# A hybrid decoder layer on one core: x also loaded feature-major, the inverse norm spread by a transpose, projection weights laid out by block

## The chip, the cores and the metric

The kernel runs on one core of one Trainium2 chip. The core has five engines with a queue of instructions each: TensorE (PE, matmuls and transposes, writes to PSUM), VectorE (DVE), ScalarE (ACT), GpSimd (POOL), and SyncE (SP), which here issues the transfers. They wait for each other by semaphores. The metric is the device time of one execution in microseconds, median of several; lower is better.

## The reference

One layer with 1024 tokens and 16 learned meta tokens in front of them, model width 1024, float32. Only its beginning is touched:

```python
h = jnp.concatenate([meta, x], axis=1)
u = rmsnorm(h, attn_norm_w[l])          # x * rsqrt(mean(x*x) + eps) * w
proj = u @ w_in[l]
gq, gk, gv, gz, gb, ga, fq, fk, fv, ff = jnp.split(proj, IN_SPLITS, axis=-1)
...                                     # gated DeltaNet group, forgetting attention group
h = h + jnp.concatenate([o_gdn, o_fox], axis=-1) @ w_out[l]
h = h + swiglu(rmsnorm(h, ffn_norm_w[l]), w_gate[l], w_up[l], w_down[l])
```

## The kernel before

Each large product is made of three fast matmuls. A float32 operand is split into a high half (a cast by ACT, line 163) and a low half (the source minus the high half, a subtraction by DVE, line 164); `mm3` (lines 197 to 199) adds high x high, high x low and low x high for each of the eight 128-row blocks k of the contraction, so one output tile takes 24 matmuls.

The first stage makes the normed input u, feature-major and split (`uh`, `ul`: 128 partitions x 8 blocks x 1040 columns), and beside it one projection that needs tokens on the output's partitions: 256 columns of the z gate and 8 gate columns, `z1`. It goes over eight tiles of 128 tokens (t = 0 to 7), then the 16 meta tokens (t = -1). For each tile `load_norm` loads 128 rows of x, and `norm_to` works on them:

- ACT squares the rows and sums along them (line 251), DVE scales and adds eps (line 212, called the statistic here), POOL raises to the power -0.5 (line 213);
- DVE multiplies the rows by the inverse norm and the norm's weight, which lies broadcast over the partitions in `nwb` (line 254, `xn`);
- PE transposes `xn` in eight 128x128 pieces into two PSUM banks (line 261), and for each bank (half 0: k = 0 to 3, half 1: k = 4 to 7) ACT casts and DVE subtracts into `uh` and `ul`.

`proj_tm` then runs the 24 z matmuls of the tile. DVE copies the 8 gate columns (line 312), ACT applies Silu to the 256 z columns (line 301), POOL multiplies by a weight (line 302), SP stores the result. `zg` is the product for the meta tokens, 8 columns wide.

`win_block` loads 256 or 264 columns of the input projection's weights in two transfers of four blocks k each, rows of 1 KB, and splits each of the two (`whi`, `wlo`). After the first stage a loop over pairs of heads loads the gk, gq and gv blocks and runs `proj_fm`, 128 columns of weights stationary against 348 or 346 tokens (`pj_k` and so on); `xlds` (the x loads) and `casts` (the last cast and subtraction of each norm) order the gk weights behind the norm.

The program's text order is a priority: the framework places instructions in each engine's queue by it and by a model of their times, and each queue then runs in order. So matmuls of two tiles can stand interleaved in PE's queue. `tc.issue_after(ins)` puts an instruction behind `ins` in the queue of the engine that runs `ins`; it adds no semaphore. Twenty warm-up products of a matrix of ones (line 133, 40 matmul instructions) come first on PE.

## Time and profile before

| | us |
|---|---|
| median of three runs | 1322.56 |
| lowest and highest run | 1321.23, 1324.68 |
| profiled execution, first to last instruction | 1318.3 |
| what lies around that span, against the median | 4.3 |
| last meta product of the first stage on PE starts | 46.63 |
| first matmul of the unbroken run of the next projection starts | 46.90 |

The profiled execution is one run, seen from inside; its span has no time of its own beside it but the runs' median. In the rows of the profile a group's idle time stands behind a bar with what ended it; in the order of instructions each row has start, duration, engine, line, operation, output, inputs and shape. SPq is SP's queue of transfers; PEld the loading of stationary operands, beside the matmuls.

### The profile page before, as it was taken

How to read it: one execution, taken by the hardware profiler on the slowest of the kernel's cores; microseconds unless marked ns; L12 is line 12 of the kernel's file. 1: busy time of each engine (PE TensorE's matmuls, PEld its weight loads, DVE VectorE, ACT ScalarE, POOL GpSimd, SP SyncE). 2: the span in 40 equal slices, each digit the busy share in tenths (PEclk: the TensorE clock that was granted, in tenths of full speed). 3: DMA queues.
4: the chain of work that ended last, by engine and by line, in shares of the span. 5: the costliest groups of instructions: out<-in, count | busy, mean ns of one | idle time of the engine just before them, and what ended most of it. 6: DMA issues, size and time to landing. Idle time of an engine off the chain costs nothing.

```text
span 1318.3 us, 20034 instructions
## 1 busy us (share of the span) xinstructions
PE 1296.8 (98%) x7442; PEld 1132.9 (86%) x7442; DVE 856.0 (65%) x1525; ACT 546.2 (41%) x918; POOL 390.6 (30%) x348
## 2 busy tenths in 40 slices
PE   8999999999999999999999999999999999999997
PEld 8999999899999988887778888888888888888886
DVE  6665789676237578996897665566566665355644
ACT  5543434232223367885553332333323343333332
POOL 2211423601023321113432644554334453010301
PEclk9999999999999999999999999999999999999999
DMA  6331743774479597647444555534454557955513
GB/s 228 98 107 38 213 134 115 215 219 144 150 241 330 180 245 207 163 118 233 166 138 137 180 176 181 172 128 155 156 169 146 176 203 261 402 178 191 210 63 128
DMA packets 184777, 233.88 MB, mean 177 GB/s; under 512 B 19121, under 2 KB 136873, under 8 KB 181865
## 3 DMA queue, kind: packets, MB, share of 16 engines
q1 hardware_dynamic: 181704, 223.70, 52.7%
q0 software_dynamic: 2976, 8.92, 2.2%
q8 instruction: 58, 0.95, 0.3%
q14 instruction: 39, 0.31, 0.1%
HBM read 154.91 MB, written 77.67 MB: 176 GB/s over the span
## 4 chain that ended last, share of the span: by engine, by line
PE 82%; DVE 6%; DMA 5%; issue 3%; ACT 2%; POOL 1%; SPq 1%; POOLq 0%; DVEq 0%; ACTq 0%
PE xp L1545 9%; PE yp L1545 7%; PE gb L1379 5%; PE gd L1379 5%; PE ud L1379 5%; PE ub L1379 5%; PE ga L1379 4%; PE ua L1379 4%; PE pj_fk L207 4%; PE pj_fq L207 4%; PE pt L1012 2%; PE ge L1379 2%; PE ue L1379 2%; PE fv L207 2%; PE wog L207 2%
## 5 line engine op out<-in xcount | busy, mean ns | idle before, releaser
L164 DVE TENSOR_TENSOR al_p<-ra_p,ah_p 128x2048 fp32r<-128x2048 f32 (+1 forms) x21 | 46.6, 2221 | 94.0 <-ACT ah_p L163 94.0
L163 ACT CAST ah_p<-ra_p 128x2048 fp32r<-128x2048 f32 (+1 forms) x21 | 37.1, 1766 | 105.8 <-PE xp L1545 48.5
L1545 PE MATMUL xp<-wh_p,ah_p 128*128 128x512 f32 (+1 forms) x187 | 70.6, 377 | 0.7 <-DVE hs L1572 0.7
L1545 PE MATMUL xp<-wl_p,ah_p 128*128 128x512 f32 (+1 forms) x187 | 70.5, 377 | 0.0
L1545 PE MATMUL xp<-wh_p,al_p 128*128 128x512 f32 (+1 forms) x187 | 70.5, 377 | 0.0
L1432 POOL TENSOR_TENSOR gzw<-gzw,uzt 128x512 f32<-128x512 f32 x11 | 18.4, 1675 | 153.8 <-DVE uzt L1423 127.6
L1432 POOL TENSOR_TENSOR gxy<-gxy,uxy 128x512 f32<-128x512 f32 x22 | 39.0, 1772 | 67.2 <-DVE uxy L1423 48.2
L1379 PE MATMUL gb<-uh_p,w_g_p 128*128 128x512 f32 x176 | 57.8, 390 | 0.0
L1379 PE MATMUL gd<-uh_p,w_g_p 128*128 128x512 f32 x176 | 57.8, 389 | 0.0
L1379 PE MATMUL ub<-uh_p,w_u_p 128*128 128x512 f32 x176 | 57.8, 389 | 0.0
L1379 PE MATMUL ud<-uh_p,w_u_p 128*128 128x512 f32 x176 | 57.8, 389 | 0.0
L985 ACT ACTIVATE pr<-pr,sm 128x144 f32<-128x144 f32 (+3 forms) x64 | 50.6, 792 | 16.9 <-DVE sm L980 16.6
L164 DVE TENSOR_TENSOR w_u_p<-raw_u,w_u_p 128x512 fp32r<-128x512 f32 x42 | 42.8, 1018 | 21.6 <-ACT w_u_p L163 21.4
L164 DVE TENSOR_TENSOR pl<-pt,ph 128x512 fp32r<-128x512 f32 (+1 forms) x96 | 51.2, 553 | 2.2 <-ACT ph L163 1.6
L1379 PE MATMUL ga<-uh_p,w_g_p 128*128 128x512 f32 x160 | 52.5, 389 | 0.0
L1379 PE MATMUL ua<-uh_p,w_u_p 128*128 128x512 f32 x160 | 52.5, 389 | 0.0
L163 ACT CAST ph<-pt 128x512 fp32r<-128x512 f32 (+1 forms) x96 | 45.4, 474 | 14.7 <-PE pt L1012 13.9
L1545 PE MATMUL yp<-wl_p,ah_p 128*128 128x512 f32 x132 | 51.4, 390 | 0.0
L1545 PE MATMUL yp<-wh_p,ah_p 128*128 128x512 f32 x132 | 51.4, 389 | 0.0
L1545 PE MATMUL yp<-wh_p,al_p 128*128 128x512 f32 x132 | 51.4, 389 | 0.0
L164 DVE TENSOR_TENSOR wl_p<-rw_p,wh_p 128x2048 fp32r<-128x2048 f32 (+1 forms) x21 | 46.9, 2235 | 3.4 <-ACT wh_p L163 3.4
L1012 PE MATMUL pt<-ident,pr 128*128 128x128 f32 x288 | 48.1, 276 | 0.0
(638 smaller groups left out, 4272.3 us busy)
## 6 DMA issues: line engine op xcount, KB each, us to landing
ra_p<-ao_p SPq DMA_DIRECT2D x14, 1024.0 KB
raw_g<-in_w_gate_dram SPq DMA_DIRECT2D x22, 512.0 KB
raw_u<-in_w_up_dram SPq DMA_DIRECT2D x22, 512.0 KB
raw_d<-in_w_down_dram SPq DMA_DIRECT2D x22, 512.0 KB
wt_p<-raw_d SPq DMA_DIRECT2D x33, 256.0 KB
rw_p<-wt_p SPq DMA_DIRECT2D x8, 1024.0 KB
rw_p<-in_w_down_dram SPq DMA_DIRECT2D x6, 1024.0 KB
ao_p<-gzw SPq DMA_DIRECT2D x22, 256.0 KB
```

Of the source, the lines that this page charges most:

```text
L163: cast = nc.scalar.copy(dst_hi, src)
L164: tail[0] = (cast, nc.vector.tensor_sub(dst_lo, src, dst_hi.bitcast(F32)))
L207: nc.tensor.matmul(dst, a, b, start=first, stop=last)
L985: nc.scalar.activation(pr[:, :n], pr[:, :n], AF.Exp, bias=sm[:, np_ - 1:np_], scale=-1.0, accum_out=rsum[:, h, j:j + 1])
L1012: nc.tensor.transpose(pt[:rows_k, P * j:P * j + P], pts[j][0][:, c0:c0 + rows_k], ident)
L1379: nc.tensor.matmul(dst, a[:, c], b[:, k], start=(first and k == 0 and i == 0), stop=(k == 3 and i == 2), skip_group_check=not first)
L1432: last_mul[0] = G.tensor_tensor(gs[d], gs[d], us[d], op=ALU.mult)
L1545: nc.tensor.matmul(dst[:, n_], a[:, f, c], b[:, f, n_], start=(first and i == 0 and n == 0), stop=(i == NF - 1 and n == 2), skip_group_che ...
```

## The change

The host passes more and other layouts. x also comes as `x_t`, for each tile of 128 tokens feature-major (128 partitions x 8 blocks x 128 tokens), the meta tokens as `meta_t`, the norm's weight as eight columns, `attn_norm_w_t`. `w_in` comes as one flat array in the order in which blocks are used, so that a transfer of `win_block` reads one run of 4096 or 4224 bytes for each partition.

`norm_to` no longer makes `xn` nor transposes it. It still squares the token-major rows for the norm. PE transposes the column of inverse norms, broadcast over 128 columns, so that a PSUM tile `pr` holds the inverse norm of each token along the columns, the same in each partition. DVE then makes, for each k, feature-major x times the weight's column times `pr` (128x128 for a tile), and the halves are split from that. Tiles 4 and 5, and 6 and 7, are normed as pairs (128x256). The norm of the next tile or pair is called from inside the z matmuls (`mm3_behind`): after `cut` of them, its transpose is put behind the last one on PE, and the rest behind the transpose. Tile 0 takes its products with low weights last. Explicit orders put the square behind a cast of the tile ahead, the statistic behind a subtraction, the multiplies behind the tile ahead's last subtraction, and the second half of the z weights behind tile 0's.

```diff
@@ -28,6 +28,8 @@
 EPS = 1e-6
 WMAX = 1056
 GQ, GK, GV, GZ, FQ, FK, FV = 0, 512, 1024, 1536, 2056, 2568, 3080
+WIN = tuple((c, 256) for c in range(0, 1792, 256)) + ((1792, 264),) + tuple(
+    (c, 256) for c in range(2056, 3336, 256)) + ((3336, 264),)
 TCH = ((0, 348), (348, 346), (694, 346))
 GRP = 4
 LV0 = (76.0, 119.0)
@@ -95,12 +97,11 @@
 
 
 @with_exitstack
-def tile_hymba_layer(ctx, tc, x, meta, attn_norm_w, w_in, conv_w, a_log, dt_bias, gdn_norm_w,
+def tile_hymba_layer(ctx, tc, x, meta, x_t, meta_t, anw_t, attn_norm_w, w_in, conv_w, a_log, dt_bias, gdn_norm_w,
                      fgate_b, w_out, ffn_norm_w, w_gate, w_up, w_down, final_norm_w, out):
     nc = tc.nc
-    x, out, w_in, conv_w = x[0], out[0], w_in[0], conv_w[0]
+    x, out, conv_w = x[0], out[0], conv_w[0]
     w_out, w_gate, w_up, w_down = w_out[0], w_gate[0], w_up[0], w_down[0]
-    w_in_v = w_in.rearrange("(k p) n -> p k n", p=P)
 
     const = ctx.enter_context(tc.tile_pool(name="const", bufs=1))
     dram = ctx.enter_context(tc.tile_pool(name="dram", bufs=1, space=bass.MemoryType.DRAM))
@@ -182,11 +183,16 @@
 
     parts_n = [1]
 
-    def win_block(c0, n, name):
+    def win_block(c0, n, name, behind=None):
         ws = ([], [])
         for i in range(2):
-            k0 = KT // 2 * i
-            hl = load_w([(w_in_v[:, k0:k0 + KT // 2, c0:c0 + n], KT // 2 * n)], f"{name}_{i}")
+            k0, m = KT // 2 * i, KT // 2 * n
+            o = P * KT * c0 + P * m * i
+            src = w_in[o:o + P * m].rearrange("(p m) -> p m", m=m)
+            with ExitStack() as es:
+                for ins in behind if behind and i else ():
+                    es.enter_context(tc.issue_after(ins.ins))
+                hl = load_w([(src, m)], f"{name}_{i}")
             for o, t in zip(ws, hl):
                 o.extend(t[:, n * k:n * k + n] for k in range(KT // 2))
         return ws
@@ -197,6 +203,19 @@
             nc.tensor.matmul(dst, lh, rh, start=(first and i == 0), stop=False)
             nc.tensor.matmul(dst, lh, rl, start=False, stop=False)
             nc.tensor.matmul(dst, ll, rh, start=False, stop=(last and i == n - 1))
+
+    def mm3_behind(dst, pairs, cut, hook, lo_last):
+        ops = [[(lh, rh), (lh, rl), (ll, rh)] for lh, ll, rh, rl in pairs]
+        if lo_last:
+            h = len(ops) // 2
+            ops = ops[:h] + [[o[0] for o in ops[h:]], [o[2] for o in ops[h:]], [o[1] for o in ops[h:]]]
+        ops = [o for g in ops for o in g]
+        ins = None
+        for i, (a, b) in enumerate(ops):
+            if hook and i == cut:
+                ins = hook(mm)
+            with tc.issue_after(ins.ins) if ins else nullcontext():
+                mm = nc.tensor.matmul(dst, a, b, start=i == 0, stop=i == len(ops) - 1)
 
     od = PeOrder()
 
@@ -237,40 +256,70 @@
     pre = ExitStack()
     xp = pre.enter_context(tc.tile_pool(name="xp", bufs=3))
     xc = pre.enter_context(tc.tile_pool(name="xc", bufs=1))
-    nwb = xc.tile([P, D], F32, name="nwb")
-    x0 = xp.tile([P, D], F32, tag="xt", bufs=5, name="xt_0")
-    nc.sync.dma_start(x0, x[0:P])
-    nc.sync.dma_start(nwb, attn_norm_w[0].partition_broadcast(P))
-
     pows, xlds, casts = [], [], []
-
-    def norm_to(src, rows, wb, hi, lo, col, pool, nm):
-        junk = pool.tile([P, D], F32, tag="junk", name=f"jk_{nm}")
-        st = pool.tile([P, 4], F32, tag="st", name=f"st_{nm}")
-        with tc.issue_after(casts[-2][0].ins) if len(casts) > 2 else nullcontext():
-            nc.scalar.activation(junk[:rows], src[:rows], AF.Square, accum_out=st[:rows, 0:1])
-        pows.append(inv_rms(st[:rows, 2:3], st[:rows, 0:1], 1, 1.0 / D, st[:rows, 1:2]))
-        xn = pool.tile([P, D], F32, tag="xn", name=f"xn_{nm}")
-        nc.vector.scalar_tensor_tensor(xn[:rows], src[:rows], st[:rows, 2:3], wb[:rows],
-                                       op0=ALU.mult, op1=ALU.mult)
+    x_q, halves_ = {}, []
+
+    def load_x(t, n=1):
+        xg = xp.tile([P, n, KT, P], F32, tag=f"xg{n}", bufs=4 - n, name=f"xg_{t}")
+        if t < 0:
+            xg = xg.rearrange("p n k c -> p (n k c)")[:, :KT * NM].rearrange("p (n k c) -> p n k c", n=1, k=KT)
+        xts = [xp.tile([P, D], F32, tag="xt", bufs=6, name=f"xt_{t + i}") for i in range(n)]
+        lds = [(xts[0][:NM], meta), (xg[:, 0], meta_t)] if t < 0 else [
+            (xts[i], x[P * (t + i):P * (t + i) + P]) for i in range(n)] + [(xg[:, i], x_t[t + i]) for i in range(n)]
+        for d, src in lds:
+            with tc.issue_after(xlds[-1].ins) if xlds else nullcontext():
+                xlds.append(nc.sync.dma_start(d, src))
+        x_q[t] = xts, xg
+
+    load_x(0)
+    wct = xc.tile([P, KT], F32, name="wct")
+    nc.sync.dma_start(wct, anw_t)
+
+    def norm_to(t, behind=None):
+        col, rows = tok_cols(t)
+        xts, xg = x_q.pop(t)
+        n = len(xts)
+        pr = ps_t(f"pr_{t}")
+        un = xp.tile([P, KT, 2 * P], F32, tag="un", bufs=2, name=f"un_{t}")
+        if t < 2:
+            order = halves_[1:] if t < 0 else casts or [None]
+        else:
+            order = (casts[-2], halves_[0]) if t == 4 else tuple(halves_)
+        for i, xt in enumerate(xts):
+            st = xp.tile([P, 4], F32, tag="st", bufs=4, name=f"st_{t + i}")
+            if rows < P:
+                nc.gpsimd.memset(st, 1.0)
+            ahead = order[i]
+            with tc.issue_after(ahead[0].ins) if ahead else nullcontext():
+                nc.scalar.activation(un[:rows, 4 * i:4 * i + 4].rearrange("p k c -> p (k c)"), xt[:rows], AF.Square,
+                                     accum_out=st[:rows, 0:1])
+            with tc.issue_after(ahead[1].ins) if ahead else nullcontext():
+                pows.append(inv_rms(st[:rows, 2:3], st[:rows, 0:1], 1, 1.0 / D, st[:rows, 1:2]))
+            with tc.issue_after(behind.ins) if behind else nullcontext():
+                last_pr = nc.tensor.transpose(pr[:, P * i:P * i + P], st[:, 2:3].to_broadcast([P, P]), ident)
+        prv = pr[:, :rows * n].rearrange("p (n c) -> p n c", n=n)
+        un = un[:, :, :rows * n]
+        cols = slice(col, col + rows * n)
         for g in range(2):
-            pt = ps_t(f"pt_{nm}_{g}")
-            pv = pt.rearrange("p (a b) -> p a b", a=4)[:, :, :rows]
-            for i in range(4):
-                k = 4 * g + i
-                nc.tensor.transpose(pv[:, i, :], xn[:rows, P * k:P * k + P], ident[:rows, :rows])
-            split_dst = (hi[:, 4 * g:4 * g + 4, col:col + rows], lo[:, 4 * g:4 * g + 4, col:col + rows])
-            split(split_dst[0], split_dst[1], pv)
+            ks = slice(4 * g, 4 * g + 4)
+            for k in range(4 * g, 4 * g + 4):
+                with tc.issue_after(casts[-1][1].ins) if casts else nullcontext():
+                    nc.vector.scalar_tensor_tensor(un[:, k].rearrange("p (n c) -> p n c", n=n), xg[:, :, k],
+                                                   wct[:, k:k + 1], prv, op0=ALU.mult, op1=ALU.mult)
+            split(uh[:, ks, cols], ul[:, ks, cols], un[:, ks])
+            halves_[g:] = [tail[0]]
         casts.append(tail[0])
+        return last_pr
 
     def tok_cols(t):
         return (0, NM) if t < 0 else (NM + P * t, P)
 
-    def proj_tm(t, w, c0, n, name, tag=ps_mm):
+    def proj_tm(t, w, c0, n, name, cut=0, hook=None):
         col, rows = tok_cols(t)
-        acc = tag(name)
-        mm3(acc[:rows, :n], [(uh[:, k, col:col + rows], ul[:, k, col:col + rows],
-                              w[0][k][:, c0:c0 + n], w[1][k][:, c0:c0 + n]) for k in range(KT)])
+        acc = ps_mm(name)
+        mm3_behind(acc[:rows, :n], [(uh[:, k, col:col + rows], ul[:, k, col:col + rows],
+                                     w[0][k][:, c0:c0 + n], w[1][k][:, c0:c0 + n]) for k in range(KT)],
+                   cut, hook, t == 0)
         return acc
 
     def proj_fm(w, m0, c0, n, name):
@@ -284,14 +333,6 @@
     nc.gpsimd.memset(gt[:, NT], 0.0)
     nc.gpsimd.memset(fr[:, NT], 0.0)
     zp = pre.enter_context(tc.tile_pool(name="zp", bufs=2))
-    def load_norm(t):
-        rows = NM if t < 0 else P
-        if t:
-            xt = xp.tile([P, D], F32, tag="xt", bufs=5, name=f"xt_{t}")
-            xlds.append(nc.sync.dma_start(xt[:rows], meta if t < 0 else x[P * t:P * t + P]))
-        else:
-            xt = x0
-        norm_to(xt, rows, nwb, uh, ul, 0 if t < 0 else NM + P * t, xp, f"a{t}")
 
     gnw = gpool.tile([P, P], F32, name="gnw")
 
@@ -302,16 +343,21 @@
         nc.gpsimd.tensor_tensor(zt, zt, gnw[:, None, :].broadcast_to([P, 2, P]), op=ALU.mult)
         nc.sync.dma_start(rec_d[t, :, 7, h0:h0 + 2], zt)
 
-    w = None
+    norm_to(0)
+    w = win_block(GZ + 256, 264, "z1", casts[0])
+    casts[0] = tail[0]
+    for t in (1, 2, 3):
+        load_x(t)
+    nc.sync.dma_start(gnw, gdn_norm_w[0].partition_broadcast(P))
     for t in range(NT):
-        load_norm(t)
-        if w is None:
-            w = win_block(GZ + 256, 264, "z1")
-            nc.sync.dma_start(gnw, gdn_norm_w[0].partition_broadcast(P))
-        acc = proj_tm(t, w, 0, 264, f"z1_{t}")
+        if t in (0, 1):
+            load_x(2 * t + 4, 2)
+        elif t == 2:
+            load_x(-1)
+        nxt = {0: (1, 18), 1: (2, 18), 2: (3, 18), 3: (4, 18), 5: (6, 6), 6: (-1, 18)}.get(t)
+        acc = proj_tm(t, w, 0, 264, f"z1_{t}", *((nxt[1], lambda mm: norm_to(nxt[0], mm)) if nxt else ()))
         nc.vector.tensor_copy(gt[:, t], acc[:, 256:264])
         gate_out(t, acc, zp, "zt", 2)
-    load_norm(-1)
     acc = proj_tm(-1, w, 256, 8, "zg")
     nc.vector.tensor_copy(gt[:NM, NT], acc[:NM, :8])
     pre.close()
@@ -557,7 +603,7 @@
         kqs = [gp.tile([P, 2, T], F32, tag="kq", bufs=3, name=f"kq_{2 * hp + i}") for i in range(2)]
         vts = [gp.tile([P, T], F32, tag="vt", bufs=2, name=f"vt_{2 * hp + i}") for i in range(2)]
         with ExitStack() as es:
-            for ins in (xlds[-1], *casts[6]) if not hp else ():
+            for ins in (xlds[-1], *casts[5]) if not hp else ():
                 es.enter_context(tc.issue_after(ins.ins))
             w = win_block(GK + c, 256, f"gk{hp}")
         for i in range(2):
...
@@ -1646,8 +1692,14 @@
 
     nc = bacc.Bacc("TRN2", target_bir_lowering=False, num_devices=1, dynamic_dma_scratch_size=1024)
     arrays, args = {}, []
+    laid = dict(inputs)
+    laid["x_t"] = np.asarray(inputs["x"]).reshape(NT, P, KT, P).transpose(0, 3, 2, 1)
+    laid["meta_t"] = np.asarray(inputs["meta_tokens"]).reshape(NM, KT, P).transpose(2, 1, 0)
+    wi = np.asarray(inputs["w_in"])[0].reshape(2, KT // 2, P, -1)
+    laid["w_in"] = np.concatenate([wi[i, :, :, c:c + n].transpose(1, 0, 2).ravel() for c, n in WIN for i in range(2)])
+    laid["attn_norm_w_t"] = np.asarray(inputs["attn_norm_w"]).reshape(KT, P).T
     for name in _INS:
-        a = np.ascontiguousarray(inputs[name])
+        a = np.ascontiguousarray(laid[name])
         arrays[f"in_{name}_dram"] = a
         args.append(nc.dram_tensor(f"in_{name}_dram", a.shape, mybir.dt.from_np(a.dtype), kind="ExternalInput").ap())
     for i, (shape, dtype) in enumerate(_OUTS):
```

More of the change, by code (lines that the diff above doesn't have):

```diff
@@ L1633, in tile_hymba_layer @@
         ubc.close()
-_INS = ["x", "meta_tokens", "attn_norm_w", "w_in", "conv_w", "a_log", "dt_bias", "gdn_norm_w", "fgate_b",
+_INS = ["x", "meta_tokens", "x_t", "meta_t", "attn_norm_w_t", "attn_norm_w", "w_in", "conv_w", "a_log", "dt_bias", "gdn_norm_w", "fgate_b",
         "w_out", "ffn_norm_w", "w_gate", "w_up", "w_down", "final_norm_w"]
```

## The prediction

> **What bounds the kernel now.** I read the summary first, then the busy time by windows over the first stage, then the order of instructions in time there.
>
> ```profile
> span 1318.3 us, 20034 instructions
> PE 1296.8 (98%) x7442; PEld 1132.9 (86%) x7442; DVE 856.0 (65%) x1525; ACT 546.2 (41%) x918; POOL 390.6 (30%) x348
> ```
> PE is busy for all but 21.5 us of the span. The change touches the first stage, where x is normed and the last 264 z and gate columns are projected, and the layout of weights loaded later. So only what moves PE's start on the next projection (pj_k) can move the end; behind it PE is full and the rest shifts as one block.
>
> ```profile
> 14.00:16.00 2.00, 0.95 (x9) 0.85 (x8) 1.41 (x4) 0.80 (x4) 0.86 (x2) 1.00 0.65 234
> 16.00:18.00 2.00, 1.04 (x8) 0.71 (x6) 2.00 (x3) 1.86 (x4) 0.39 (x1) 1.00 0.97 282
> 25.00:30.00 5.00, 5.00 (x44) 5.00 (x43) 4.07 (x9) 3.47 (x8) 1.32 (x3) 1.00 0.37 127
> 35.00:40.00 5.00, 5.00 (x45) 5.00 (x43) 4.35 (x7) 4.40 (x8) 2.06 (x3) 1.00 0.08 26
> 40.00:45.00 5.00, 4.12 (x34) 3.61 (x34) 3.29 (x8) 1.14 (x4) 2.99 (x2) 1.00 0.29 59
> ```
> The columns are window, length, busy PE, PEld, DVE, ACT, POOL, PE clock, DMA share and GB/s. From 20 to 40 us PE is full: the norm runs a tile ahead, and transposes fill PE between z matmuls. DVE is busy 80 to 87% of that time, so the second limit is close behind the first. PE has holes at 14 to 18 and 40 to 45 us.
>
> ```profile
> 45.47 0.28 PE L197 MATMUL z<-whi_z,uh 128*128 128x264 f32 x1
> 45.59 0.29 PE L198 MATMUL z<-wlo_z,uh 128*128 128x264 f32 x1
> 45.71 0.28 PE L199 MATMUL z<-whi_z,ul 128*128 128x264 f32 x1
> 46.39 0.17 PE L199 MATMUL zg<-whi_z,ul 128*16 128x8 f32 x1
> ...
> 46.63 0.17 PE L199 MATMUL zg<-whi_z,ul 128*16 128x8 f32 x1
> 46.90 0.32 PE L197 MATMUL pj_k<-uh,whi_gk 128*128 128x348 f32 x1
> 47.05 0.32 PE L198 MATMUL pj_k<-ul,whi_gk 128*128 128x348 f32 x1
> ```
> Two z matmuls start 0.12 us apart, two of pj_k about 0.16, and nine of zg (the meta rows) in 0.24, 0.027 each. Three pj_k matmuls ran before the one at 46.90, so the old first stage ends, in terms of pj_k's start, at 46.90 - 3 x 0.16 = **46.4 us**. That is the number to beat.
>
> **The change, part by part.** Durations of the parts, from the groups of the first stage:
>
> ```profile
> 7.93 1.09 PE L261 MATMUL pt_a<-ident,xn_a 128*128 128x128 f32 x8
> ```
> ```profile
> L254 DVE SCALAR_TENSOR_TENSOR xn_a<-xt,st_a,nwb 128x1024 f32<-128x1024 f32 x7 | 11.3, 1616 | 4.1 <-POOL st_a L213 3.4 <-DMA xt_-1_585<-in_meta_tokens_dram 0.7
> L164 DVE TENSOR_TENSOR ul<-pt_a,uh 128x512 fp32r<-128x512 f32 x16 | 10.5, 679 | 0.4 <-ACT uh L163 0.4
> L163 ACT CAST uh<-pt_a 128x512 fp32r<-128x512 f32 x16 | 9.1, 583 | 6.7 <-PE pt_a L261 6.6
> L251 ACT ACTIVATE jk_a<-xt 128x1024 f32<-128x1024 f32 x7 | 7.4, 1062 | 1.1 <-DMA xt<-in_x_dram 0.9
> L251 ACT ACTIVATION_READ_ACCUMULATOR jk_a<-xt 128x1 f32 x7 | 1.3, 191 | 0.0
> L164 DVE TENSOR_TENSOR wlo_gk<-raw_gk,whi_gk 128x1024 fp32r<-128x1024 f32 x2 | 2.4, 1205 | 0.0
> L163 ACT CAST whi_gk<-raw_gk 128x1024 fp32r<-128x1024 f32 x2 | 2.0, 1039 | 0.0
> ```
> The first row is the order in time, eight transposes of tile 0; the others are groups with count, busy time and mean. Removed: 64 transposes (and the meta's 8) on PE, about 0.11 us each, some 7 to 8 us; and one xn of 1.6 us per tile. Added: one transpose per tile of the broadcast inverse norm, and eight multiplies of x, feature-major, by weight column and spread norm in PSUM. Their nearest rows are multiplies with a PSUM input later in the kernel:
>
> ```profile
> 128.54 0.35 DVE L498 SCALAR_TENSOR_TENSOR ktna<-pq,nbr,ktna 128x128 f32<-128x128 f32 x1
> 128.81 0.34 DVE L500 SCALAR_TENSOR_TENSOR gce<-pq,rk,gce 128x128 f32<-128x128 f32 x1
> 130.36 0.34 DVE L500 SCALAR_TENSOR_TENSOR gce<-pq,rk,gce 128x128 f32<-128x128 f32 x1
> ```
> Eight of them start at a pitch of 0.26 us, so a tile's eight end 2.16 us after the first starts. For a pair of tiles (128x256) I add the measured slope, (1.205 - 0.679)/512 per element, 0.13 us: pitch 0.39, eight in 3.2 us. DVE thus gets dearer per tile (2.1 against 1.6), PE cheaper.
>
> What decides is order. The hook puts the next tile's transpose behind the 18th z matmul of this tile, and matmuls 15 to 18 need this tile's second low half (sub); the next tile's multiplies need that transpose. So nothing of DVE's work runs a tile ahead any more. One round of a single tile, from its first multiply at 0:
> - multiplies 0 to 2.16; the cast of half 0 (after the fourth) 1.17 to 1.75;
> - the square of the next tile is ordered behind that cast on ACT: with its read 1.25 us, to 3.0. The cast of half 1 waits for it: 3.0 to 3.55;
> - sub of half 0 in DVE's gap, sub of half 1 3.6 to 4.3;
> - PE: matmuls 15 to 18 and the transpose, 4 x 0.12 + 0.27 and handovers of 0.05, to 5.1. The six z matmuls queued behind the transpose on PE run beside DVE; the gate columns and Silu of the tile wait for those and are off this path.
>
> **A round is 5.15 us**, where the old one was about 3.8 (24 x 0.12 + 8 x 0.11). Bounds: 4.8 with sub 0 early and no square in the way (matmuls 3 to 18 still take 16 x 0.12), 5.5 with the gate copy, Silu or square late. PE idles 1.5 to 2 us in each.
>
> The start. Warm-up matmuls hold PE, so the early norm (POOL's result at 6.55) doesn't help the transpose:
>
> ```profile
> 1.20 6.80 PE L133 MATMUL warm<-ones 128*128 128x128 f32 x40 [1.20 <-POOL ones L130]
> 6.00 0.55 POOL L213 TENSOR_TENSOR st_a<-st_a,mhalf 128x1 f32<-128x1 f32 x1 [3.11 <-DVE st_a L212]
> 7.73 1.07 ACT L163 CAST whi_z<-raw_z 128x1056 fp32r<-128x1056 f32 x1 [2.07 <-DMA raw_z<-in_w_in_dram]
> 9.22 1.07 ACT L163 CAST whi_z<-raw_z 128x1056 fp32r<-128x1056 f32 x1
> 11.71 1.06 ACT L251 ACTIVATE jk_a<-xt 128x1024 f32<-128x1024 f32 x1 [0.93 <-DMA xt<-in_x_dram]
> 12.89 0.15 DVE L212 TENSOR_SCALAR st_a<-st_a 128x1 f32<-128x1 f32 x1 [0.43 <-ACT jk_a L251]
> 13.13 0.55 POOL L213 TENSOR_TENSOR st_a<-st_a,mhalf 128x1 f32<-128x1 f32 x1 [6.57 <-DVE st_a L212]
> ```
> Multiplies of tile 0 from 8.15. DVE then has 2.1, two z low halves (1.25 each, pitch 1.15) and two subs (pitch 0.6); the second z low half is ordered behind the tile's subs: 8.15 + 2.1 + 1.15 + 0.6 + 0.6 + 1.25 = 13.85. The statistic of tile 1 is ordered behind that; with 0.15, POOL's 0.55, handovers and the transpose its first multiply comes at **15.1** (the old one started behind POOL's 13.13 + 0.55). Bounds 14.0 (z low half not in the way) and 15.4.
>
> Data:
>
> ```profile
> 10.00:12.00 2.00, 1.64 (x11) 1.44 (x12) 2.00 (x4) 1.07 (x3) 0.00 (x0) 1.00 1.04 422
> ```
> ```profile
> 1.25 0.42 SPq L243 DMA_DIRECT2D nwb<-in_attn_norm_w_dram  x1
> ```
> x0, its feature-major copy and the z weights are the same bytes as x0, the broadcast norm weight and the z weights before, so z weights land near 7.7 and 9.2, and x1 near 11.5. x comes twice, 8.4 MB, from a queue that moved 234 to 422 GB/s in busy windows of this stage; at 280 GB/s the last copy lands near 36 us, before its use at 38. SP issues nine more loads at about 0.4 us each, ahead of the gnw load and the gate stores, which nothing here waits for soon; one load waits for a buffer that tile 0's multiplies free near 10 us, with five issued ahead of it to cover. The small column load (32 bytes a partition) has no row: nothing if it lands by 8.1, 1.1 us if it comes behind the z weights; I take nothing, since it is issued before them.
>
> The rounds: tiles 1, 2, 3 give 15.1 + 3 x 5.15 = **30.5** for the first pair. There: eight multiplies 3.2, casts of 1.04, subs of 1.2 (pitch 1.14), squares of the next pair between the casts; sub 1 ends at 6.3, the statistic and POOL take to 7.2, and PE fills with tile 4 and the first six matmuls of tile 5: the next pair starts 7.65 later, **38.2** (bounds 7.2 and 8.75, the latter if tile 5's six matmuls all run behind tile 4's). Last pair: sub 0 ends at 4.35; then 44 z matmuls x 0.12, the meta's transpose and zg (24 at 0.027, 0.65): 10.5 more. The meta's norm and the gk low halves (2.4 us of DVE) are covered by tile 7's matmuls; uncovered they cost up to 1. pj_k starts at **48.7** (bounds of this leg 9.9 and 11.4).
>
> The sum is 48.7 - 46.4 = **+2.3 us**. All low ends give 45.5 (-0.9), all high ends 52.0 (+5.6). The profiled execution spans 1318.3; the median of the runs is 1322.56, and the 4.3 us around the span stay, so the forecast is 1322.56 + 2.3 = **1324.9 us**, own range 1321.6 to 1328.2.
>
> Weights laid out by block: the same bytes in rows of 4 KB in place of 1 KB. Later no PE wait in the list of waits is on a weight load, so this is worth nothing; at most a fraction of a us at the start.
>
> **The clock.** PE's gaps grow, and one row shows what a gap did:
>
> ```profile
> 238.00:240.00 2.00, 0.17 (x2) 0.00 (x0) 2.00 (x4) 0.00 (x0) 1.52 (x1) 1.00 0.42 140
> 240.00:242.00 2.00, 1.67 (x11) 1.52 (x11) 2.00 (x6) 1.84 (x2) 2.00 (x2) 0.77 0.50 66
> 242.00:244.00 2.00, 2.00 (x11) 2.00 (x10) 2.00 (x4) 1.27 (x4) 2.00 (x2) 0.50 0.51 69
> 246.00:248.00 2.00, 2.00 (x19) 2.00 (x18) 0.42 (x2) 0.37 (x1) 1.84 (x3) 1.00 0.62 173
> ```
> ```profile
> 240.33 0.27 PE L466 MATMUL prk<-ident,rk 128*8 128x128 f32 x1 [2.16 <-POOL rk L463]
> ```
> After 2.16 us idle PE ran at half clock for some 4 us; 11 matmuls in 2 us instead of 19 lose 0.8 us per 2 us, 1.6 in all. The holes at 14 to 18 us, shorter, left it at 1.00. [...]
>
> **Rivals.**
> - *The clock drops* ahead of both pairs. There PE waits about 1.8 us for cast 0 and, after two to four matmuls, 1.3 us for sub 0: as near to the row's 2.16 as to the harmless holes. Price 2 x 1.6 = 3.2: 1328.1, slower. It decides from a gap of some 2 us on.
> - *DVE alone bounds*, no link through PE: the transpose is late in no round, each round loses 0.85, the pair too: 4 x 0.85 = 3.4 less, 1321.5. Against it: the transpose is behind the 18th matmul by an explicit order.
> - *PE alone bounds* as from 20 to 40 us before: 192 x 0.12 + 9 x 0.11 + 0.65 = 24.7 after a first z matmul at 10.4, pj_k at 35.1, 11.3 less: 1311.3. It needs DVE's two subs, multiplies, statistic and gate copy, 2 x 0.68 + 2.1 + 2 x 0.15 = 3.8, under 2.9 per tile, which isn't so. A case midway to no change (the scheduler finds work for the gaps) gives 1317.
> - *It doesn't do what it says*: the second x copy is late. At 200 GB/s the last copy lands at 49 us, +10. The rows of this stage speak against it.
>
> **Chances.** The chain as summed 0.60 (of it 0.46 within 0.3% and 0.14 above); the clock or a late x 0.22, slower; DVE alone 0.05, within; PE alone or half-way 0.13, faster. A measurement of this kernel can tell about 0.3%, 4 us, from no change. So faster 0.13, same 0.51, slower 0.36. The range takes in the clock and half of the half-way cases: 1318.0 to 1330.0.
>
> **What would show it.** First pj_k matmul near 48.7; eight multiplies at a pitch of 0.26 and rounds near 5 us, with PE idle 1.5 to 2 us in each between 15 and 30 us; clock 1.00 throughout (0.5 somewhere before 45 us speaks for the rival). I am wrong if multiplies of a tile start before the tile ahead has its second sub (rounds under 4 us), if multiplies take under 0.2 us, or if the time moves behind pj_k's start.

## The result, and the profile after

| | before | after |
|---|---|---|
| median of six runs each, us | 1322.15 | 1331.05 |
| lowest and highest run, us | 1321.23, 1324.68 | 1327.53, 1336.31 |
| span of the profiled execution, us | 1318.3 | 1331.4 |
| the next projection's start (pj_k), as worked out in the prediction | 46.4 | 55.7 |
| busy PE, DVE in that execution, us | 1296.8, 856.0 | 1298.7, 859.6 |

The ratio after to before is 1.007, 95% interval 1.0054 to 1.0085: slower, by some 9 us. The forecast was 1324.9, its range ended at 1330.0.

The page of the changed kernel, first part (busy time, share of the span, instructions by engine):

```profile
span 1331.4 us, 19950 instructions
PE 1298.7 (98%) x7379; PEld 1134.0 (85%) x7379; DVE 859.6 (65%) x1568; ACT 546.5 (41%) x914; POOL 386.8 (29%) x349
```
PE has 63 instructions fewer, as the change intends, and yet is busy 1.9 us longer; the mean granted clock of this execution is 0.991, that of the profiled execution of before 0.998.

Out of the order of instructions in time on DVE, of the changed kernel, the rows of each norm's multiplies (start, duration, line, operation, shape, count; in brackets the idle time ahead and what ended it):

```profile
8.49 2.16 DVE L307 SCALAR_TENSOR_TENSOR un<-xg,wct,pr 128x128 f32<-128x128 f32 x8 [2.67 <-PE pr L299]
16.10 2.16 DVE L307 SCALAR_TENSOR_TENSOR un<-xg,wct,pr 128x128 f32<-128x128 f32 x8 [1.85 <-PE pr L299]
21.37 2.16 DVE L307 SCALAR_TENSOR_TENSOR un<-xg,wct,pr 128x128 f32<-128x128 f32 x8 [1.15 <-PE pr L299]
26.63 2.16 DVE L307 SCALAR_TENSOR_TENSOR un<-xg,wct,pr 128x128 f32<-128x128 f32 x8 [1.15 <-PE pr L299]
33.45 3.22 DVE L307 SCALAR_TENSOR_TENSOR un<-xg,wct,pr 128x256 f32<-128x256 f32 x8 [2.76 <-PE pr L299]
44.26 3.22 DVE L307 SCALAR_TENSOR_TENSOR un<-xg,wct,pr 128x256 f32<-128x256 f32 x8
53.26 1.22 DVE L307 SCALAR_TENSOR_TENSOR un_-1_519<-xg_-1_308,wct,pr_-1_518 128x16 f32<-128x16 f32 x8
```
Each row is the eight multiplies of one tile, one pair of tiles or (the last) the meta tokens. They last 2.16 us, and 3.22 for a pair, as forecast. From the second to the third row and on to the fourth it is 5.27 and 5.26 us, also as forecast, and each waits for the transpose (`pr`) that stands behind the tile ahead's 18th matmul: the serial chain is there. But the step from 26.63 to 33.45 is 6.8 us, and the pair takes 10.8 to the next pair instead of 7.65.

The order on PE, same kernel, from 36 us on:

```profile
36.29 0.39 PE L218 MATMUL z<-whi_z,uh 128*128 128x264 f32 x1 [2.02 <-ACT uh L164]
...
37.94 0.59 PE L218 MATMUL z<-whi_z,ul 128*128 128x264 f32 x1 [0.88 <-DVE ul L165]
38.32 0.42 PE L218 MATMUL z<-whi_z,uh 128*128 128x264 f32 x1
38.54 0.42 PE L218 MATMUL z<-wlo_z,uh 128*128 128x264 f32 x1
...
56.38 0.40 PE L204 MATMUL pj_k<-ul,whi_gk 128*128 128x348 f32 x1
```
Two z matmuls start 0.22 us apart here, against 0.12 before. The last row opens the unbroken run of pj_k, with four of its matmuls run earlier: 56.38 - 4 x 0.16 = 55.7 us.

The list of waits of PE in the first 60 us, same kernel (us in total, times, longest):

```profile
PE z L218 <- ACT uh L164: 7.9, 6, 2.0
PE z L218 <- DVE ul L165: 3.6, 6, 0.9
```
Six times PE waits for a tile's first cast and six times for its first low half, 11.5 us in all. These are the gaps that the prediction put at 1.5 to 2 us a round. How the clock goes beside them shows best in windows of 3.41 us, as long as the trace's first stretch at half clock (13.11 to 16.52 us). Window, length, busy PE, PEld, DVE, ACT, POOL, granted clock of PE, DMA share, GB/s; the changed kernel:

```profile
9.70:13.11 3.41, 1.42 (x7) 1.01 (x8) 3.41 (x8) 3.05 (x4) 0.00 (x0) 1.00 1.03 423
13.11:16.52 3.41, 3.41 (x17) 3.41 (x17) 1.56 (x4) 0.21 (x2) 0.55 (x1) 0.50 0.77 269
16.52:19.94 3.42, 2.00 (x13) 1.57 (x13) 2.98 (x11) 2.46 (x5) 0.64 (x2) 1.00 0.95 377
19.94:23.35 3.41, 2.21 (x19) 2.00 (x17) 2.26 (x9) 0.77 (x2) 0.87 (x1) 1.00 1.03 420
23.35:26.76 3.41, 2.92 (x22) 2.71 (x23) 1.82 (x6) 2.84 (x6) 1.52 (x2) 1.00 1.01 401
26.76:30.18 3.42, 1.69 (x12) 1.26 (x11) 3.07 (x13) 2.18 (x4) 1.18 (x2) 1.00 1.05 347
30.17:33.59 3.42, 3.42 (x18) 3.42 (x17) 0.66 (x2) 0.24 (x1) 0.27 (x1) 0.50 0.56 214
33.59:37.00 3.41, 1.40 (x10) 1.03 (x8) 3.41 (x10) 1.95 (x3) 0.77 (x2) 1.00 0.12 38
37.00:40.41 3.41, 2.53 (x12) 2.48 (x12) 2.24 (x4) 2.55 (x6) 1.33 (x3) 0.50 0.00 0
40.41:43.83 3.42, 3.42 (x18) 3.42 (x17) 0.00 (x0) 0.00 (x0) 0.45 (x1) 0.50 0.12 38
43.83:47.24 3.41, 2.70 (x22) 2.49 (x22) 3.09 (x9) 1.43 (x2) 0.75 (x1) 1.00 0.12 38
```
Four of these windows stand at a granted clock of 0.50, the others at 1.00. Each stretch at half clock follows a window in which PE was busy 1.42, 1.69 or 1.40 us, about half or less; those with 2.00 and 2.21 us were followed by 1.00. The three half-clock windows that PE fills hold 17 or 18 matmuls; at the 0.12 us from start to start of full clock one would hold some 28 (an estimate, 3.41/0.12).

What lies behind pj_k is the same in both: span less pj_k's start is 1271.9 us before and 1275.7 after, and the order of instructions on PE, ACT and DVE is the same from pj_q on, the projection after pj_k; its first matmul starts at 71.1 us before and at 80.5 after. The 3.8 us between these are mostly the draw of the profiled execution: a run's time is its span plus 1.7 us (1333.09 and 1331.4 for the profiled run of after), so the profile of before, at 1318.3, stands for 1320.0, some 2 us under that kernel's median. The rest is not tied to the change: the kernel of before with only the weights laid out anew (the first experiment) took 1275.1 there, without any of the late half-clock stretches (one in the trace of before, from 241.1 us on, two in that of after, from 252.0 and 381.7). So the loss of 9 us is the first stage's: 55.7 - 46.4 = 9.3.

### The profile page after: what moved, and what is told of

Its sections match the earlier page's. It is cut to its first block, busy times and chain, and to the rows that moved or that the text cites. A ratio compares the mean times of both kernels' runs of the same rounds, so it can differ in the third digit from the quotient of the medians.

```text
span 1331.4 us, 19950 instructions
## 1 busy us (share of the span) xinstructions
PE 1298.7 (98%) x7379; PEld 1134.0 (85%) x7379; DVE 859.6 (65%) x1568; ACT 546.5 (41%) x914; POOL 386.8 (29%) x349
## 4 chain that ended last, share of the span: by engine, by line
PE 81%; DVE 7%; DMA 6%; issue 2%; POOL 1%; SPq 1%; ACT 1%; POOLq 0%; DVEq 0%; ACTq 0%
PE xp L1591 8%; PE yp L1591 7%; PE gb L1425 4%; PE ud L1425 4%; PE gd L1425 4%; PE ub L1425 4%; PE ua L1425 4%; PE ga L1425 4%; PE pj_fq L226 4%; PE pj_fk L226 4%; PE pt L1058 2%; PE ue L1425 2%; PE ge L1425 2%; PE po L1080 1%; PE fv L226 1%
## 5 line engine op out<-in xcount | busy, mean ns | idle before, releaser
L165 DVE TENSOR_TENSOR w_u_p<-raw_u,w_u_p 128x512 fp32r<-128x512 f32 x42 | 41.9, 998 | 21.6 <-ACT w_u_p L164 21.5
L1425 PE MATMUL ga<-uh_p,w_g_p 128*128 128x512 f32 x160 | 52.5, 389 | 0.0
L1425 PE MATMUL ua<-uh_p,w_u_p 128*128 128x512 f32 x160 | 52.5, 389 | 0.0
L164 ACT CAST ph<-pt 128x512 fp32r<-128x512 f32 (+1 forms) x96 | 45.4, 474 | 14.6 <-PE pt L1058 13.8
```

What stands on the lines that cost most here:

```text
L164: cast = nc.scalar.copy(dst_hi, src)
L165: tail[0] = (cast, nc.vector.tensor_sub(dst_lo, src, dst_hi.bitcast(F32)))
L1425: nc.tensor.matmul(dst, a[:, c], b[:, k], start=(first and k == 0 and i == 0), stop=(k == 3 and i == 2), skip_group_check=not first)
```

## The experiments

Theories at the start: the chain (one round after the other through transpose, multiplies, split and 18 matmuls) costs some us by itself; the clock, halved by the gaps of the chain, costs the rest. Rivals: the weights' new layout, and the multiplies' length. In all kernels below the end of the first stage is pj_k's start, worked out as before. In kernels with added lines, line 218 (z) is 226, 299 (`pr`) is 311, 307 (multiplies) is 319.

**The layout of the weights alone**, put into the kernel of before:

```diff
...
-            hl = load_w([(w_in_v[:, k0:k0 + KT // 2, c0:c0 + n], KT // 2 * n)], f"{name}_{i}")
...
+            src = w_in[o:o + P * m].rearrange("(p m) -> p m", m=m)
+            hl = load_w([(src, m)], f"{name}_{i}")
...
```


> The kernel before with nothing but the projection weights laid out by block. Theory (the loss is made in the first stage, by rounds that wait for each other and by clock drops in their gaps): no change, 1322 us within 2, later stages shifted by nothing. Rival (part of the loss comes behind the first stage, from the new weight loads meeting other transfers): 1325 to 1326, with the first pj_k matmul where it was, near 46 us.

Ratio to before 1.0002 (0.999 to 1.0014, 11 runs), pj_k at 46.3. By itself the layout costs and brings nothing, so the loss is put down to the x path.

**The gaps of PE filled** with products of a matrix of ones into a PSUM tile that nobody reads; the chain is as in the changed kernel:

```diff
+    fillb = ps_s("fill")
+    f_end, f_mid = {0: 4, 1: 4, 2: 4, 3: 9, 5: 4}, {0: 5, 1: 3, 2: 3, 3: 3, 4: 5, 6: 6}
+    def fillers(behind, n):
+        for _ in range(n):
+            with tc.issue_after(behind.ins):
+                nc.tensor.matmul(fillb[:, :P], ones, ones, start=True, stop=True)
...
+            if i == (1 if t else 0):
+                fillers(mm, f_mid.get(t, 0))
+            if i == len(ops) - 1:
+                fillers(mm, f_end.get(t, 0))
...
-    norm_to(0)
+    fillers(norm_to(0), 9)
```


> The kernel after with dummy products of a matrix of ones on PE in the gaps of the first stage, in an unused PSUM bank; nothing else is moved. Theory: the granted clock stays at 1.00 there, rounds stay near 5.2 us, the first pair starts near 31 us instead of 33.45 and pj_k near 49.5 instead of 55.7, so 1325 to 1326 us and a smaller spread of runs. Rival (the clock rows are a side show, DVE's longer norm sets the stage): the fillers change nothing or cost up to 2 us, 1331 to 1333.

In the trace the clock is 1.00 for the first 60 us. The multiplies start at 14.60, 19.84, 25.09, 30.52 and 38.67, and pj_k at 50.9: without half clock the stage still ends 4.5 us later than before. The time did not follow: 1332.94 (1326.78 to 1337.19), ratio 1.007 (1.0045 to 1.0094). The profiled execution lost elsewhere. Its windows far behind the first stage:

```profile
318.19:321.60 3.41, 2.59 (x28) 1.88 (x26) 1.61 (x4) 1.58 (x3) 0.00 (x0) 1.00 0.12 46
321.60:325.01 3.41, 3.13 (x18) 2.46 (x19) 3.16 (x8) 0.71 (x2) 1.05 (x1) 0.50 0.28 104
...
331.84:335.25 3.41, 3.41 (x13) 3.31 (x12) 0.97 (x3) 0.46 (x1) 1.05 (x1) 0.50 0.42 122
335.25:338.67 3.42, 3.42 (x23) 3.42 (x23) 0.68 (x2) 0.46 (x1) 0.00 (x0) 1.00 0.43 142
```
Half clock for four windows (321.60 to 335.25), in a stage that the change doesn't touch and that was at full clock in the traces of before and after. Rows of 64x64 matmuls stand ahead of it. Against the trace of before, PE is 6.1 us late with the same matmul at 315 us, and 12.9 us late at 354 us.

**The same kernel once more**, to see whether that stretch belongs to it:

> The kernel with the gaps filled once more, unchanged, to see whether its later stretch of half clock (321 to 335 us) comes again at that place. If it is tied to what the first stage did, it comes again between 315 and 340 us, with a span near 1331 us and a median near 1333 us. If drops fall on chance places of the later stages, the profile shows it elsewhere or not at all, with a span of 1323 to 1326 us without one; the median of the runs stays between 1327 and 1334 us. In both cases the clock is 1.00 in the first 50 us and pj_k's equivalent start 50.5 to 51.5 us.

It doesn't: windows of 5 us of this trace, the first three rows of those from 10 to 50 us, all at 1.00:

```profile
10.00:15.00 5.00, 4.54 (x33) 3.85 (x33) 4.24 (x8) 2.96 (x5) 0.55 (x1) 1.00 1.02 406
15.00:20.00 5.00, 4.71 (x37) 4.50 (x38) 3.68 (x12) 2.46 (x5) 1.51 (x2) 1.00 0.81 310
20.00:25.00 5.00, 4.70 (x39) 4.49 (x38) 3.68 (x12) 2.70 (x6) 1.24 (x3) 1.00 1.03 415
```
No half clock shows later either (1.00 in each window of 20 us up to 1320); pj_k starts at 51.6, the span is 1325.9, and span less pj_k's start is 1274.3. Yet the median of ten runs is 1331.12, ratio 1.005 (1.0029 to 1.0072); their granted clocks range from 0.992 to 0.999. So with the gaps filled the first stage is at 1.00 in both traces, and three runs in ten show the gain plainly (spans 1324.8 to 1325.9, clock 0.998 or 0.999); the others are slower at places that were not traced, two of them (1327.5 and 1330.0) although their clock is 0.998. The median of the runs is no better than the changed kernel's, and the expectation of 1325 to 1326 was missed.

**The transpose earlier in the round** (behind the 12th matmul instead of the 18th), without and with the fill:

```diff
-        nxt = {0: (1, 18), 1: (2, 18), 2: (3, 18), 3: (4, 18), 5: (6, 6), 6: (-1, 18)}.get(t)
+        nxt = {0: (1, 18), 1: (2, 12), 2: (3, 12), 3: (4, 12), 5: (6, 6), 6: (-1, 18)}.get(t)
```


> The kernel after with the transpose of the next norm behind the 12th instead of the 18th z matmul in tiles 1, 2 and 3, so that it no longer waits for the tile's second subtraction. Theory: rounds of tile 2 and 3 shrink from 5.26 to about 4.4 us, the pair's likewise, about 2.5 us less from that, and shorter gaps may spare one clock drop of 1.6 us: 1327 to 1329. If PE's link doesn't matter (DVE and ACT alone set the rounds): 1331 as after.

> Both together: fillers in the gaps and the transpose behind the 12th matmul. Theory: the two gains add, first pj_k near 47, 1322.5 to 1324 us, about the kernel before. Rival (DVE's norm sets the stage): 1329 or more.

Without the fill: 1329.42, ratio 1.0052 (1.0033 to 1.0071), pj_k 53.1; rounds are 4.5 to 4.7 us where the clock is full, but four stretches at half clock stand ahead of 50 us. With it: 1328.70, ratio 1.004 (1.0028 to 1.0053), pj_k 50.1, rounds 4.5 to 4.7, no half clock in the stage. The chain does go through the place of the transpose: 0.7 us a round, which is the six matmuls of 0.12 us that no longer stand ahead of it. What three rounds gain is in part lost at the start (tile 0's multiplies begin at 8.8 us, tile 1's at 15.6) and in the pair (8.6 us). The two gains did not add up to the 1322.5 to 1324 us that were expected.

**Two long multiplies a tile instead of eight.** One weight column serves four blocks, so this kernel leaves out three quarters of the norm's weight:

```diff
-            for k in range(4 * g, 4 * g + 4):
+            for i in range(n):
...
-                    nc.vector.scalar_tensor_tensor(un[:, k].rearrange("p (n c) -> p n c", n=n), xg[:, :, k],
-                                                   wct[:, k:k + 1], prv, op0=ALU.mult, op1=ALU.mult)
+                    nc.vector.scalar_tensor_tensor(un[:, ks, rows * i:rows * i + rows], xg[:, i, ks], wct[:, 4 * g:4 * g + 1],
+                                                   prv[:, i][:, None, :].broadcast_to([P, 4, rows]), op0=ALU.mult, op1=ALU.mult)
```


> The kernel after with two long multiplies per tile in place of eight short ones, with one column of the norm's weight for four blocks, so three quarters of the weight are left out. Theory (multiplies lie in the chain of a round): two take 1.3 instead of 2.16 us, rounds fall by about 0.8 to 4.4, a pair by 0.7, pj_k 3 to 4 us earlier, and clock drops may be fewer: 1325 to 1328. Rival (PE's link and the clock alone set the rounds): no change, 1331.

1327.05, ratio 1.0031 (1.002 to 1.0042), pj_k 49.2, rounds 4.70. The length of the multiplies is in the chain too, 0.57 us a round, but even so the stage ends later than before.

**The norm one tile ahead**, with all eight multiplies:

```diff
-            order = (casts[-2], halves_[0]) if t == 4 else tuple(halves_)
+            order = (casts[-2],) * n
...
-                with tc.issue_after(casts[-1][1].ins) if casts else nullcontext():
+                with tc.issue_after(casts[-1][1].ins) if len(casts) == 1 else nullcontext():
...
-        nxt = {0: (1, 18), 1: (2, 18), 2: (3, 18), 3: (4, 18), 5: (6, 6), 6: (-1, 18)}.get(t)
+        nxt = {0: (1, 18), 1: (2, 2), 2: (3, 2), 3: (4, 2), 4: (6, 2), 6: (-1, 18)}.get(t)
```


> The kernel after with the norm one tile ahead, as it was before the change: the next tile's transpose behind the 2nd z matmul, its square and statistic behind the tile two before, its multiplies no longer ordered behind the last subtraction. Theory (the new norm's cost is its order, a round that passes through PE, and the gaps that this leaves): DVE then sets rounds of 3.6 to 4.0 us, PE is nearly full, the clock holds at 1.00, and pj_k comes near 46, as in the kernel before: 1321 to 1324 us. Rival (the norm's more and shorter DVE instructions themselves cost the time, whatever the order): rounds stay at 5 us, 1328 to 1332.

1327.35, ratio 1.0031 (1.0017 to 1.0045), pj_k 47.5, with half clock left at 12.6 to 16.0 and 19.4 to 22.8 us. The order by which nothing of DVE's ran ahead was most of the chain's cost. The total came out higher than the expected 1321 to 1324, 4 us above before. The trace shows 1.1 of them at pj_k, and its run (1325.4) is 2 us faster than the median, so where the other runs lose the rest is not shown.

**Both: one tile ahead, and the gaps filled** (products behind tile 0's transpose, tile 0's first matmul, and tiles 0, 2 and 3):

```diff
+    f_end, f_mid = {0: 4, 2: 3, 3: 3}, {0: 5}
```


> The norm one tile ahead, as in the run-ahead kernel, and products of ones beside it that keep PE busy where that kernel's trace still had gaps followed by half the clock (8 to 12 us and 16 to 18 us). Theory of chain and clock: with neither, the granted clock is 1.00 up to 45 us and pj_k's equivalent start is 45 to 46.5 us, at or before the 46.3 us of before (the run-ahead kernel had 47.45 with the clock at 0.80 and 0.86 from 10 to 30 us); the time is then within 2 us of before, 1321 to 1325 us. Rival, that a drop which is kept away in the first stage comes in a later one instead, as the 321 to 335 us stretch of the kernel with the gaps filled suggests: the stage ends as early, but the clock drops later in the profile and the median stays at 1327 us or more. Rival that the products delay the chain: rounds longer than 5.5 us and pj_k at 48 us or later.

1324.67 against 1324.68 of before on that chip, ratio 0.9998 (0.9981 to 1.0015). The order on PE, with four pj_k matmuls run earlier:

```profile
46.63 0.41 PE L204 MATMUL pj_k<-ul,whi_gk 128*128 128x348 f32 x1
```
46.63 - 4 x 0.16 = 46.0, and the clock is 1.00 up to there. Chain and clock together are the whole loss: take both away and the kernel is back at the time of before. Against before, the medians are 1.007 and 1.0075 with neither mended, 1.007 and 1.005 with the gaps filled, 1.0031 with the order mended, and 0.9998 with both: the fill pays in the median only where the order is mended too. The kernel is not faster than before, though PE is spared 64 transposes. The sum of the eight 5 us windows from 10 to 50 us:

```profile
sum 40.00, PE 35.41 PEld 32.70 DVE 33.18 ACT 25.45 POOL 13.01; mean PE 4.43 PEld 4.09 DVE 4.15 ACT 3.18 POOL 1.63
```
DVE is busy 83% of this stretch, against 75% (29.94 us) in the same windows of before. From 8 to 47 us PE stands 3.1 us for the casts and subtractions of z, which come behind DVE's multiplies. So what PE saved is probably held up by DVE; no run tests that.

**The changed kernel twice more**, first timed, then for one trace to test what the clock goes by. In the traces so far the edges of the half-clock stretches stood a whole number of windows of one length apart: in the changed kernel's own, 13.11 to 252.03 is 70 times 3.413 us, and 13.11 to 381.73 is 108 times 3.413 us.

> The kernel after, unchanged, for a second trace and more runs. Theory: the rounds are the same to 0.1 us where the clock is 1.00, and the spread of runs (1327.5 to 1336.3 so far) goes with the clock, some 1.2 us of span for each 0.001 of mean granted clock; half-clock stretches lie in the first 60 us again, not all at the same places. Rival (drops are an accident of one trace): no half clock there.

> The changed kernel once more, to test on a fresh trace what the earlier traces suggest: the clock is granted in slots of 3.41 us on one grid per run, and the slot after one in which PE was busy under half (1.7 us) runs at half clock. From the traces of after, its repetition and four experiments with projections at half or full clock in the first stage: every slot with 1.74 us or less was followed by half clock, every one with 1.92 us or more by the full one (between them both occurred). Slot theory: the half-clock stretches of this trace begin a whole number of 3.41 us slots apart, each straight behind a slot with less than 1.92 us of PE, and no slot under 1.74 us goes without one, in the first 60 us; pj_k's equivalent start 52 to 57 us, depending on where the grid falls. Rival, a single long gap sets it off: the stretches begin within 0.3 us of the end of a gap of 1.9 us or more, off any grid, and always at the same places as in after (13, 30 and 37 us).

First: 1332.74, ratio 1.0075 (1.0056 to 1.0094), pj_k 54.1, half clock at 11.2 to 14.6 and 35.1 to 41.9. Second: 1333.41, one run, pj_k 57.1. Its windows, on the grid of its own edges (laid 0.05 us late, so that 0.99 and 0.51 stand for 1.00 and 0.50):

```profile
7.32:10.74 3.42, 1.60 (x15) 1.35 (x13) 1.78 (x7) 1.64 (x2) 0.00 (x0) 1.00 1.01 405
10.74:14.15 3.41, 1.99 (x11) 1.58 (x12) 3.41 (x6) 2.70 (x5) 0.00 (x0) 0.99 1.03 419
14.15:17.56 3.41, 3.29 (x16) 2.98 (x14) 1.97 (x8) 0.19 (x1) 0.55 (x1) 0.51 0.67 232
17.56:20.98 3.42, 2.45 (x17) 2.24 (x18) 2.28 (x7) 2.27 (x5) 1.51 (x2) 1.00 1.03 418
20.98:24.39 3.41, 1.72 (x13) 1.30 (x11) 2.88 (x11) 1.75 (x4) 0.00 (x0) 0.99 1.04 418
24.39:27.80 3.41, 3.41 (x16) 3.41 (x17) 0.80 (x2) 1.86 (x4) 1.51 (x2) 0.51 1.01 399
27.80:31.21 3.41, 1.66 (x12) 1.24 (x11) 3.00 (x12) 1.85 (x4) 0.64 (x1) 0.99 1.04 349
31.21:34.63 3.42, 3.42 (x16) 3.42 (x17) 0.70 (x2) 0.71 (x2) 1.54 (x3) 0.51 0.23 81
```
The stretches again begin whole windows apart (near 14.1, 24.3, 31.2 and 38.0), at other places than in the first trace (13.11, 30.18 and 37.0). The one at 24.3 follows a round whose longest gap was 1.20 us, and a gap of 1.93 us, up to 10.85, was followed by full clock up to 14.1. So the length of one gap does not tell where they begin in this trace; how much PE did in the window ahead tells it better, though not sharply. The bounds in the expectation were too tight: 1.60 us was not followed by half clock here, and 1.99 was (1.65 and 1.94 with the windows laid on the edges). And they can only be meant for windows at full clock: in the changed kernel's first trace one with 2.53 us at half clock (37.0 to 40.4) was followed by half clock.

**The fill only at the start and in the pairs**, the rounds of tiles 1 to 3 left with their gaps:

```diff
+    f_end, f_mid = {3: 9, 5: 4}, {0: 5, 4: 5, 6: 6}
```


> After with products of ones only at the start (tile 0) and in the two pairs; the gaps in the rounds of the single tiles 1 to 3 stay as they are (PE busy 58 to 86% of a slot there, but 1.69 us in the slot ahead of the first pair in after). Slot theory: no half clock at 10 to 16 us nor from 35 to 50 us; between 18 and 35 us at most one stretch of 3.4 us, in some runs none, so pj_k's equivalent start is 50.5 us without and about 52 us with one. If gaps of 1.1 us are enough by themselves, each round of tiles 1 to 3 shows half clock and pj_k starts at 54 us or later. The median is 1328 to 1333 us, like the kernel with all gaps filled.

1332.53, ratio 1.0072 (1.0045 to 1.01), pj_k 52.5. One stretch at half clock in the stage, where it could still come:

```profile
14.64:18.05 3.41, 1.73 (x12) 1.31 (x11) 2.97 (x12) 2.46 (x5) 0.53 (x1) 0.99 0.64 224
18.05:21.46 3.41, 3.41 (x18) 3.41 (x17) 1.10 (x4) 0.00 (x0) 0.98 (x2) 0.51 1.02 413
21.46:24.88 3.42, 2.08 (x14) 1.66 (x14) 2.98 (x10) 2.46 (x5) 0.88 (x2) 1.00 1.02 413
```
The six traces with the unchanged chain, ordered by windows at half clock ahead of pj_k:

| kernel | windows at half clock | pj_k starts, us |
|---|---|---|
| filled | 0 | 50.9 |
| filled, again | 0 | 51.6 |
| filled at start and pairs | 1 | 52.5 |
| changed kernel, again | 3 | 54.1 |
| changed kernel | 4 | 55.7 |
| changed kernel, third trace | 5 | 57.1 |

Part of the steps in this table is the start, for tile 0's multiplies begin at 7.56, 8.49 and 8.96 us in the last three rows. The price of a window shows better in single steps: from one tile's multiplies to the next 5.26 us without and 6.77 with one (third trace), into the first pair 5.43 and 6.82 (changed kernel), and from pair to pair 8.15 in the filled kernel and 10.49 to 11.46 with two. That is 1.2 to 1.7 us a window, at most half of 3.41. The three traces without fill, carried back to no window at 1.5 us each, give 49.6 to 49.7; the filled kernels end at 50.9 and 51.6, but their products add 0.7 us to the last leg (12.2 from the last pair's multiplies to pj_k, 11.5 in all three others). By these estimates the chain costs some 3 to 5 us and the clock the rest, 4 to 6 of the 9.3 us in the changed kernel's first trace.

## Why the prediction was wrong

The sign that the sum gave was right, and most of its steps held; the size failed, on two terms. The larger is the clock, put at nothing in the sum: three to five windows at half clock in the stage, 4 to 6 us in the trace above. The smaller is the legs of the pair and behind it, 1.5 us together.

- **What bounds it**: right. Only pj_k's start moves the end; what lies behind it took 1272 to 1276 us in all traces but two, which had more half clock later, and the loss is that start's.
- **The multiplies**: right, 2.16 us for eight (forecast 2.1 to 2.2) and 3.22 for a pair (3.2).
- **Tile 1's first multiply at 15.1**: 14.6 and 15.3 at full clock in the two filled traces, 16.1 in the changed kernel, behind the first half-clock window.
- **A round of 5.15 us**: the size is right, 5.27 and 5.26, the path is not. The prediction ends the round with the second subtraction and matmuls 15 to 18 behind it. One round of the changed kernel, rows of DVE and PE picked out of the order in time:

```profile
23.51 0.68 DVE L165 TENSOR_TENSOR ul<-un,uh 128x512 fp32r<-128x512 f32 x1
24.25 0.39 PE L218 MATMUL z<-whi_z,ul 128*128 128x264 f32 x1 [0.49 <-DVE ul L165]
24.79 0.69 DVE L165 TENSOR_TENSOR ul<-un,uh 128x512 fp32r<-128x512 f32 x1 [0.35 <-ACT uh L164]
25.84 0.28 PE L218 MATMUL z<-whi_z,ul 128*128 128x264 f32 x1
26.32 0.27 PE L299 MATMUL pr<-ident,st 128*128 128x128 f32 x1
```
  PE's last wait is for the first subtraction; from 24.25 on its matmuls 3 to 18 run without a gap. The 15th, at 25.84, comes 0.36 us after the second subtraction's end. This path stands in the prediction only as the lower bound of 4.8; that both come to nearly the same length is luck.
- **The first pair at 30.5**: 30.52 and 31.26 at full clock; 33.45 in the changed kernel, two half-clock windows later. That 30.52 meets the forecast is luck too: it began 0.5 us earlier, and its three steps (5.24, 5.25, 5.43) took 0.5 longer.
- **The pair's leg of 7.65**: mis-sized, 8.15 and 8.2 at full clock, inside its bounds.
- **The last leg of 10.5**: mis-sized. It took 11.5 in the changed kernel, at full clock from 43.8 us on. The prediction let tile 7's matmuls cover the meta tokens' norm and named up to 1 us if they don't. The meta's multiplies start only at 53.26: behind tile 7's last matmul, at 54.18, zg waits for the meta tokens' low half (no start from 54.33 to 54.74), and pj_k for Silu (`zt`, none from 55.04 to 55.37). These two legs make +3.8 us out of the forecast's +2.3 (30.5 + 8.2 + 11.5 - 46.4).
- **The clock**: here the prediction failed. It read the row of 2.16 us idle as a rule on the length of one gap, took the harmless holes of before as evidence for 1.00 throughout, and made the drop a rival within 0.22, for two gaps, at 3.2 us. The price of one drop, 1.6, was right; how many there are was not. No run shows the 1.00 that the sum took for this chain as it stands: it was the author's choice, and the three traces have four, three and five windows at 0.50. The same places of before in windows of 3.41 us, on that trace's grid:

```profile
12.33:15.74 3.41, 2.33 (x18) 1.97 (x17) 1.72 (x6) 2.07 (x5) 1.15 (x3) 1.00 0.81 297
15.74:19.16 3.42, 2.46 (x18) 1.92 (x17) 3.25 (x5) 2.71 (x5) 0.94 (x2) 1.00 0.92 258
...
237.59:241.00 3.41, 1.25 (x10) 0.75 (x9) 3.41 (x5) 1.25 (x2) 2.52 (x2) 1.00 0.52 137
241.00:244.41 3.41, 3.41 (x18) 3.41 (x17) 3.41 (x10) 2.27 (x4) 3.41 (x2) 0.51 0.44 60
```
  The holes at 14 to 18 us left PE busy two thirds of a window; the gap at 238 left it a third. The forecast's own round, 24 x 0.12 + 0.27 of PE in 5.15 us, with its work and gaps each in one piece, leaves some 2 us idle in a round, so a window that holds the whole gap has 1.4 us of work. By that reading the drop was the likely case and not the rival: three to five windows in three traces.
- **The other rivals.** Late x: no; the transfers are nearly idle from 33.6 us on (DMA share 0.12), ahead of the last pair. PE alone, or halfway: no; with order and gaps both mended the stage ends at 46.0. DVE alone, without the link through PE, is what that kernel comes near to: it has the time of before, where 1 us less was put down for it. The prediction read DVE as 80 to 87% busy from 20 to 40 us; in windows of 5 us it is 76 to 87%.
- **The weights' layout** at nothing: right, 1.0002. **The 4.3 us around the span**: 1.7 of it is what a run adds; the rest was the draw of the profiled execution.

Open: why kernels with the gaps filled keep a median near 1331 to 1333 although their traced first stage ends 3 to 6 us earlier. The clocks of single runs say part of it. Of the sixteen runs of the kernel with all gaps filled, the seven at 0.998 or 0.999 have spans from 1324.8 to 1330.0 us, the middle one 1325.9; that is some 3 to 5 us above the kernel of before beside them, as the chain alone would have it; the nine at 0.992 to 0.995 have 1328.8 to 1335.5. One run of the slower group was traced, and it has the half clock from 321 to 335 us. Why that comes in half of the runs, and whether it is always there, is not shown.

## What to carry to other kernels

In this kernel a serial chain between engines cost twice: by the estimates above some 3 to 5 us by its own length, and 4 to 6 us by the half clock that came behind its gaps. Before trusting "PE idles a little in each round", lay short windows over the rounds of a trace and read busy PE and the granted clock in each. Here the windows were 3.41 us long: in the first stages half clock followed each of the ten at full clock that left PE busy 1.46 us or less, and a window at half clock made its step 1.2 to 1.7 us longer. Work taken off the full engine gained nothing while the order written for the new work let nothing run ahead (ratio 1.007), and nothing either with order and gaps mended (0.9998), where the next engine, DVE, was busy 83%; that DVE then held it up is likely, not shown.
